# Branch operands, gates and summed weights laid out in DRAM in reading order; branch results added by VectorE; inputs turned beside the first out pair

## The chip, the cores and the metric

One NeuronCore of one Trainium2 chip runs the whole program. It has five engines with queues of their own: TensorE (PE in the profile, its weight loads PEld), VectorE (DVE), ScalarE (ACT), GpSimd (POOL) and SyncE (SP), and 16 DMA engines that they share. SP and POOL issue the transfers. An engine's queue runs in order: an instruction that waits holds up everything behind it. The metric is the device time of one execution in microseconds (us); less is better.

## The reference: what is computed

One layer of a streaming encoder, width 1024, over 1024 prompt frames and 32 sample frames (1056 together), in fp32:

```
z = RMSNorm(x) @ W_in                    # queries, keys, values, gates
y_A = attention(...)                     # windowed, 16 heads
y_B = HGRN2(...)                         # gated linear recurrence, 8 heads
m = sigmoid(gate_A) * (y_A @ W_brA) + sigmoid(gate_B) * (y_B @ W_brB)
x = x + RMSNorm(m @ W_out)
x = x + RMSNorm((gelu(conv3(a)) * u) @ W_down),  [a | u] = RMSNorm(x) @ W_up
x = x + (p @ W_ple) * sigmoid(x @ W_ple_gate)
```

The change touches how `y_A`, `y_B`, the gates and the branch weights get into DRAM and back, the line of `m`, the product with `W_out`, and the transposition of the per-layer input `p`.

## The kernel before

**Numbers.** Activations lie transposed: features on the 128 partitions, frames along the row. Every fp32 product is made of three reduced-precision ones. A value is split into a high part (`hi`, a cast on ScalarE) and what is left (`lo`, a subtraction on VectorE), and PE multiplies hi by hi, hi by lo and lo by hi. `split` and `halves` are these two steps. For the weights of the out projection they make `wh` and `wl` (`load_next`, lines 182 to 189); where ScalarE has time, `lo_by` can be set to "dma" and `lo` is made by ScalarE (minus the weight) and an accumulating transfer on POOL.

**Stages, in order of time.** Attention to about 365 us, the HGRN recurrence to 822, the last gates to 851, branch A (`y_A @ W_brA`) to 938, branch B to 1022.6, the out projection in two pairs to 1076 and 1127.5, the product with `W_ple`, the feed-forward part to 1840, and the end.

**The branches** use a Strassen-like scheme: instead of eight block products seven are made, from sums of blocks. `H` is 264 frames, a quarter of 1056; halves of frames, of features and of columns are named by t, h, a. The sums of activations lie in DRAM (`sa_d`, `sb_d`), the sums of weights too (`wa_d`, `wb_d`). They are made during the HGRN stage by transfers that add on arrival, issued by POOL (`block_sum`, line 1458; `a_sums`, `y_sums`, `b_sums` are 21 of them, and `yb_sum` adds the activations of B by heads). `gate_out` (line 292) writes the gates `ta_d`, `tb_d` as [128, 1056] in frame order, the HGRN output goes to `yb_d` so as well.

`a_unit(br, ph, c)` does one column block of 128: in phase 0 the products i = 0, 1, 2, in phase 1 i = 3 to 6, each with 24 matmuls of 128 x 264 into a PSUM tile `st`. These are 34 steps for A (some are halves) and 28 for B; `beside(n)` runs what `during(step, ...)` has put beside a step: operand loads (`a_load`), splits (`a_split`), weight pieces. `both(...)` puts them behind what ScalarE and VectorE have got already; otherwise a scheduler chooses each engine's order. For i = 2, 4, 5, 6 a result comes out: VectorE subtracts (L1662), and multiplies by the gate (L1664). A's results are written to `mx_d` by POOL (L1669). B's are added to them by an accumulating transfer `ta<-mx_d` (L1671), and three steps later `out_parts` splits the sum into the operands `Ra`, `Rb` of the out projection (L228, L229). Only the last three results have their addend loaded (`ma_load`) and added by VectorE (L1666).

**The out projection.** `W_out` comes in 8 blocks of columns, twice: `p` 0 and 1 are two pairs of frame quarters. `block` makes a bank `mm` with 24 matmuls (L205 to L207), `z_out` scales it and sums its squares (L1796 to L1802). Beside the first pair `early_parts` prepares weights of later stages (`pw`, stored to `pw_d` by POOL). Beside the second pair the first pair's norm and residual are made (L1849 on), and `p_cols` turns `p`: 12 pieces of 88 frames, two PE transposes each into two banks `tr`; after every third piece the two banks are split into `pc` (L228, L229). There are two `tr` banks, so the next group's first transpose waits until these splits have read them. `ple_product` uses the `pc` tiles after the second pair.

## Time and profile before

| | us |
|---|---|
| median of 3 runs | 1959.74 (1958.93 to 1960.01) |
| profiled execution | 1956.43 |
| its span, first to last instruction | 1954.7 |
| mean granted TensorE clock | 0.998 of full |

| stage (us from the span's start) | length | PE busy | DVE busy | ACT busy | POOL busy |
|---|---|---|---|---|---|
| last gates, 822 to 851 | 29.00 | 28.37 | 12.48 | 12.80 | 4.33 |
| second out pair, 1076 to 1127.5 | 51.50 | 48.89 | 40.60 | 33.63 | 6.79 |
| `W_ple` product, 1127.5 to 1160 | 32.50 | 31.86 | 23.59 | 21.11 | 8.61 |

The branches and the first out pair are shown in the prediction. A matmul is named by what it writes and reads (`st<-oa,wt`: into the PSUM tile `st` from the activation `oa` and the weight `wt`); operands of A are `oa`, of B `ob`, a raw weight piece is `wa`, its split `wt`. `DMA_DIRECT2D` on POOL is the issue of a transfer, not the transfer. [...]

### The profile page before, as it was taken

Reading aid. Unit: us, or ns where it says so; the run is one execution under the profiler, and the core shown is the slowest. Engines: PE = TensorE matmul, PEld = TensorE weight load, DVE = VectorE, ACT = ScalarE, POOL = GpSimd, SP = SyncE. Lnnn points to the kernel's source line nnn. Section 1 sums busy time; section 2 is a strip of 40 time slices with the busy share of each in tenths; the row PEclk is TensorE's granted clock in tenths of the full one; section 3 lists DMA queues with packets and bytes.
Section 4 is the critical chain, followed back from the end, with each engine's and each line's share of the span. In section 5 each row is a group of like instructions: output and inputs, shape, how many; then the busy total and the mean of one; then the engine's idle time right before and its main releaser. Section 6 shows DMA issues by size and latency. Waiting matters only on the chain.

```text
span 1954.7 us, 38121 instructions
## 1 busy us (share of the span) xinstructions
PE 1921.2 (98%) x14523; PEld 1901.4 (97%) x14523; DVE 1466.1 (75%) x3189; ACT 1027.3 (53%) x2212; POOL 343.9 (18%) x464
## 2 busy tenths in 40 slices
PE   8999999999999999999999999999999999999998
PEld 8999999999999999999989999999999999999998
DVE  6777777788888888666675878788777786768862
ACT  7667777666666666553435663333333336534432
POOL 2111211010101001101111124354554410000000
PEclk9999999999999999999999999999999999999999
DMA  8544543455547354499988583656988357755442
GB/s 269 149 114 122 132 128 92 143 113 138 146 113 176 111 119 95 126 306 301 279 196 271 175 271 107 184 150 185 178 169 198 107 175 235 220 183 155 117 133 84
DMA packets 332300, 325.62 MB, mean 167 GB/s; under 512 B 17654, under 2 KB 293017, under 8 KB 332118
## 3 DMA queue, kind: packets, MB, share of 16 engines
q1 hardware_dynamic: 290533, 234.61, 39.0%
q0 software_dynamic: 41456, 88.53, 20.6%
q8 instruction: 114, 1.87, 0.4%
q14 instruction: 69, 0.56, 0.1%
q10 hardware_dynamic: 128, 0.06, 0.0%
HBM read 232.58 MB, written 132.20 MB: 187 GB/s over the span
## 4 chain that ended last, share of the span: by engine, by line
PE 39%; issue 5%; DVE 3%; DMA 2%; ACT 1%; POOL 0%; ACTq 0%; POOLq 0%; DVEq 0%; SPq 0%
PE st L2330 7%; PE st L2329 7%; PE st L2328 7%; PE st L2452 4%; PE st L2454 4%; PE st L2453 4%; PE st L205 2%; PE st L206 2%; PE st L207 2%; DMA pw_d<-pw 1%; DMA ta<-mx_d 1%; DVE wt L1996 0%; PE mm L205 0%; PE mm L206 0%; PE mm L207 0%
## 5 line engine op out<-in xcount | busy, mean ns | idle before, releaser
L2328 PE MATMUL st<-op,wt 128*128 128x264 f32 x1232 | 348.8, 283 | 2.8 <-ACT Sp L2339 1.4
L2330 PE MATMUL st<-op,wt 128*128 128x264 f32 x1232 | 349.7, 284 | 0.0
L2329 PE MATMUL st<-op,wt 128*128 128x264 f32 x1232 | 347.7, 282 | 0.0
L2328 PEld LDWEIGHTS st<-op,wt 128*128 128x128 f32 x1232 | 231.2, 188 | 4.6 <-ACT Sp L2339 2.0
L2329 PEld LDWEIGHTS st<-op,wt 128*128 128x128 f32 x1232 | 231.4, 188 | 0.0
L2330 PEld LDWEIGHTS st<-op,wt 128*128 128x128 f32 x1232 | 230.8, 187 | 0.0
L2452 PE MATMUL st<-dop,wt 128*128 128x264 f32 x616 | 174.5, 284 | 1.5 <-ACT S L2467 1.5
L2454 PE MATMUL st<-dop,wt 128*128 128x264 f32 x616 | 174.3, 283 | 0.0
L2453 PE MATMUL st<-dop,wt 128*128 128x264 f32 x616 | 173.9, 282 | 0.0
L1995 ACT CAST wt<-wu 128x512 fp32r<-128x512 f32 x126 | 76.0, 618 | 178.7 <-POOL wu L2004 71.0
L205 PE MATMUL mm<-La,wh 128*128 128x384 f32 (+1 forms) x480 | 158.2, 330 | 0.0
L206 PE MATMUL mm<-Lb,wh 128*128 128x384 f32 (+1 forms) x480 | 155.3, 324 | 0.5 <-DVE Lb L782 0.5
L207 PE MATMUL mm<-La,wl 128*128 128x384 f32 (+1 forms) x480 | 154.9, 323 | 0.1
L1996 DVE TENSOR_TENSOR wt<-wu,wt 128x512 fp32r<-128x512 f32 x126 | 86.4, 694 | 44.9 <-ACT wt L1995 44.9
L2452 PEld LDWEIGHTS st<-dop,wt 128*128 128x128 f32 x616 | 115.6, 188 | 2.2 <-ACT S L2467 1.9
L2453 PEld LDWEIGHTS st<-dop,wt 128*128 128x128 f32 x616 | 115.7, 188 | 0.0
L2454 PEld LDWEIGHTS st<-dop,wt 128*128 128x128 f32 x616 | 115.4, 188 | 0.0
L2101 ACT CAST wt<-wd 128x512 fp32r<-128x512 f32 (+1 forms) x84 | 49.0, 586 | 91.3 <-PE st L2454 69.8
L206 PEld LDWEIGHTS mm<-Lb,wh 128*128 128x128 f32 x480 | 90.4, 189 | 1.6 <-DVE Lb L782 1.4
L207 PEld LDWEIGHTS mm<-La,wl 128*128 128x128 f32 x480 | 90.2, 188 | 0.5 <-DVE wl L757 0.5
L205 PEld LDWEIGHTS mm<-La,wh 128*128 128x128 f32 x480 | 90.2, 188 | 0.2 <-ACT La L779 0.2
L1120 PE MATMUL G<-La,wt 128*128 128x288 f32 x288 | 90.4, 314 | 0.0
(609 smaller groups left out, 6276.7 us busy)
## 6 DMA issues: line engine op xcount, KB each, us to landing
wu<-in_w_up_dram SPq DMA_DIRECT2D x42, 512.0 KB
wu<-in_w_in_dram SPq DMA_DIRECT2D x36, 512.0 KB
w_d<-in_w_down_dram POOLq DMA_DIRECT2D x24, 704.0 KB, 8.5
a_d<-Up SPq DMA_DIRECT2D x22, 528.0 KB
wr<-in_w_in_dram SPq DMA_DIRECT2D x21, 512.0 KB
s_d<-sm SPq DMA_DIRECT2D x40, 264.0 KB
dop<-s_d SPq DMA_DIRECT2D x16, 528.0 KB
wr<-in_w_out_dram SPq DMA_DIRECT2D x16, 512.0 KB
```

The lines of the kernel that those rows point to most:

```text
L205: E.matmul(ps, wh, a, start=first and n == 0, stop=False)
L206: E.matmul(ps, wh, b, start=False, stop=False)
L207: E.matmul(ps, wl, a, start=False, stop=last and n == len(ks) - 1)
L1120: E.matmul(o, wh, x[0][k], start=first and k == 0, stop=False, skip_group_check=True)
L1995: S.copy(t[:, 0], src)
L1996: V.tensor_tensor(t[:, 1], src, t[:, 0].bitcast(F32), op=ALU.subtract)
L2328: E.matmul(o, wh, xh, start=first and k == 0, stop=False, skip_group_check=True)
L2329: E.matmul(o, wh, xl, start=False, stop=False, skip_group_check=True)
L2330: E.matmul(o, wl, xh, start=False, stop=k == 3, skip_group_check=True)
L2452: E.matmul(o, wh, xh_, start=first and k == 0, stop=False, skip_group_check=True)
L2453: E.matmul(o, wh, xl_, start=False, stop=False, skip_group_check=True)
L2454: E.matmul(o, wl, xh_, start=False, stop=k == ng - 1, skip_group_check=True)
```

## The change

Five parts.

1. Layouts. `ya_d`, `yb_d`, `ta_d`, `tb_d`, `sa_d`, `sb_d`, `wa_d`, `wb_d` are indexed in the order in which the branches read them, so that a load takes one run per partition: 4224 B for an operand instead of 4 x 1056, 2112 for a gate instead of 2 x 1056, 2048 for a summed weight piece instead of 4 x 512. Writers pay with more pieces: `gate_out` and the HGRN output write two transfers instead of one, and the weight sums of each branch become 26 transfers instead of 8.
2. Results of B. No accumulating transfer: every result's addend `ma` is loaded by SP about three results ahead, VectorE adds it, and the split stands one step later instead of three.
3. `W_out`. The first two blocks are loaded at steps 55 and 57 and split at 58 and 59 with `lo` by ScalarE and an accumulating transfer; later blocks as before. In the first pair, what `early_parts` makes stands behind what ScalarE and VectorE have by then.
4. The last result. It is made in two halves of frames; the second half now stands behind the first and behind what the queues hold.
5. `p_cols` moves from the second out pair to the first. Groups 2 and 3 come first, go to DRAM (`pc_d`) and are reloaded late in the second pair.

```diff
-    ya_d = dp.tile([P, 8, T], F32, name="ya_d")
-    ta_d = [dp.tile([P, T], F32, name=f"ta_d{i}") for i in range(8)]
+    ya_d, yb_d = (dp.tile([P, 2, 2, 2, 4, H], F32, name=f"y{x}_d") for x in "ab")
+    ta_d, tb_d = ([dp.tile([P, 2, 2, H], F32, name=f"t{x}_d{i}") for i in range(8)] for x in "ab")
...
-    wa_d, wb_d = ({o: dp.tile([P, 4, 512], F32, name=f"w{x}_d{o}") for o in (1, 3, 4, 6)} for x in "ab")
-    sa_d, sb_d = ({o: dp.tile([P, 4, 2, H], F32, name=f"s{x}_d{o}") for o in (1, 3, 4, 5)} for x in "ab")
+    wa_d, wb_d = ({o: dp.tile([P, 4, 4, P], F32, name=f"w{x}_d{o}") for o in (1, 3, 4, 6)} for x in "ab")
+    sa_d, sb_d = ({o: dp.tile([P, 2, 4, H], F32, name=f"s{x}_d{o}") for o in (1, 3, 4, 5)} for x in "ab")
...
-            dma(dst[:, o:o + n], t[:, :n])
+            for a, e in PIECES[g]:
+                q = a // H
+                dma(dst[:, q % 2, q // 2, a % H:a % H + e - a], t[:, a - o:e - o])
...
-        for n, (dst, (o, src, acc)) in enumerate(sums):
-            at(26 + 15 * n // 2, block_sum, dst[o][:], src, acc)
+        def weight_sums(d, v):
+            parts = ((3, 0, 0, 0), (4, 0, 1, 0), (1, 0, 0, 0), (6, 1, 0, 0), (3, 0, 1, 1), (4, 1, 1, 1))
+            r = [(d[o][:, c], v[:, a, h, c], acc) for o, a, h, acc in parts for c in range(4)]
+            return r + [(d[1][:], d[4][:], 1), (d[6][:], d[1][:], 1)]
...
+        for n, a in enumerate(y_sums + weight_sums(wa_d, av) + weight_sums(wb_d, bv)):
+            at(26 + 17 * n // 6, block_sum, *a)
...
-                    for z_ in (slice(0, 1), slice(1, 2)) if last and i == 6 else (sl,):
+                    def result(z_):
...
-                        if last:
-                            V.tensor_tensor(g, g, ma_a[i][:, z_], op=ALU.add)
-                            out_parts(c + 4 * a, h, ta, range(z_.start, z_.stop))
+                        if br:
+                            V.tensor_tensor(g, g, ma[:, z_], op=ALU.add)
+                            if last and i > 4:
+                                out_parts(c + 4 * a, h, ta, range(z_.start, z_.stop))
+                    if last and i == 6:
+                        result(slice(0, 1))
+                        both(result, slice(1, 2))
+                    else:
+                        result(sl)
...
-                    elif not last:
-                        gdma(ta[:], mx_d[:, 2 * a + h, c], accum_op=ALU.add)
-                        during(n_s[0] + 3, both, out_parts, c + 4 * a, h, ta)
+                    else:
+                        if not (last and i > 4):
+                            during(n_s[0] + 1, both, out_parts, c + 4 * a, h, ta)
+                        if mixes:
+                            mix_load()
...
-        during(58, prefetch)
-        during(59, both, load_next)
+        for n in range(2):
+            during(32 + n, mix_load)
+            during(55 + 2 * n, raw_next)
+            during(58 + n, both, load_next)
...
-        g, i = divmod(n, 3)
+        i, g = n % 3, (n // 3 + 2) % 4
...
+            if g > 1:
+                dma(pc_d[g - 2][:], xs[:].bitcast(F32))
...
-                if p and c > 1:
+                if p == 0 and c > 1:
                     with behind(E):
-                        p_cols(2 * c + g - 6)
+                        p_cols(2 * c + g - 4)
```

Where it moves instructions, on the engines that the prediction speaks of:

VectorE at the end of branch B, before the change. `ac` and `e` are results, `st` the PSUM tile of the last product, the numbers behind the names tell tiles apart; L1662 with 128x264 is the subtraction of one half of the last result, L229 makes `Rb`.

```order
L1662 TENSOR_TENSOR ac_13080<-st_12940,Rb__12080 128x264
L1666 TENSOR_TENSOR ta_12901<-ta_12901,ma_12937 128x528
L1664 SCALAR_TENSOR_TENSOR ta_12935<-ta_12935,ac_13080 128x264
L1662 TENSOR_TENSOR ac_13086<-st_12940,Rb__12080 128x264
L229 TENSOR_TENSOR Rb_12148<-ta_12901,Ra_12147 128x264
L229 TENSOR_TENSOR Rb_12150<-ta_12901,Ra_12149 128x264
```

And with the change, the same place (L1667 is the subtraction, L1669 the gate, L1671 the add, L227 `Rb`):

```order
L1671 TENSOR_TENSOR ta_13043<-ta_13043,ma_13077 128x528
L227 TENSOR_TENSOR Rb_12262<-ta_13043,Ra_12261 128x264
L227 TENSOR_TENSOR Rb_12264<-ta_13043,Ra_12263 128x264
L227 TENSOR_TENSOR Rb_12657<-ta_13006,Ra_12656 128x264
L227 TENSOR_TENSOR Rb_12659<-ta_13006,Ra_12658 128x264
L1667 TENSOR_TENSOR e_13218<-st_13088,Rb__12194 128x264
L1669 SCALAR_TENSOR_TENSOR ta_13079<-ta_13079,e_13218 128x264
L1671 TENSOR_TENSOR ta_13079<-ta_13079,ma_13151 128x264
L227 TENSOR_TENSOR Rb_12657<-ta_13079,Ra_12656 128x264
L1667 TENSOR_TENSOR e_13224<-st_13088,Rb__12194 128x264
```

The second read of `st`, which frees the PSUM tile, moved from the second place behind the first read to the fourth, and both moved behind four `Rb` of the two results before.

VectorE in the first out pair with the change, where the second group of `p` pieces is split. `pw` are early weight parts (L2052 their `lo`), `wl` an out weight, `sqz` the sums of squares, `pc` the turned `p` from the banks `tr`.

```order
L2052 TENSOR_TENSOR pw_13307<-rs_13305,pw_13306 128x1024
L184 TENSOR_TENSOR wl_13729<-wr_13726,wh_13728 128x1024
L1809 TENSOR_TENSOR sqz_13243<-sqz_13243,sq_13635 128x264
L2052 TENSOR_TENSOR pw_13306<-rs_13305,pw_13306 128x1024
L227 TENSOR_TENSOR pc_13646<-tr_13559,pc_13646 128x264
L227 TENSOR_TENSOR pc_13646<-tr_13560,pc_13646 128x264
```

The last two rows are new in this place; before, they stood in the second pair, behind the residual steps L1850 and L1913.

## Prediction

> **What bounds the kernel now.** The page comes first. Its first line says that TensorE (PE) works through 98% of the span, so no other engine's total matters; only what makes PE wait can be won.

> ```profile
> PE 1921.2 (98%) x14523; PEld 1901.4 (97%) x14523; DVE 1466.1 (75%) x3189; ACT 1027.3 (53%) x2212; POOL 343.9 (18%) x464
> ```

> Second, the list of who waited for whom, for PE alone and from 840 to 1165 us, where the change works (branch A to about 938, branch B to 1022.6, out projection to 1127.5). The columns are the total wait in us, times, longest.

> ```profile
> PE tr L1952 <- DVE pc L229: 2.5, 1, 2.5
> PE mm L205 <- ACT Ra L228: 2.5, 1, 2.5
> PE st L1640 <- DVE ac L1662: 2.3, 2, 1.5
> PE st L1642 <- DVE ob L1558: 1.5, 1, 1.5
> PE st L1640 <- ACT as L1649: 1.4, 1, 1.4
> ...
> PE st L1640 <- DVE R L1651: 0.9, 1, 0.9
> PE st L1640 <- ACT gt L297: 0.8, 1, 0.8
> PE tr L1822 <- DVE pc L229: 0.6, 1, 0.6
> PE st L1640 <- DVE ac L1654: 0.5, 1, 0.5
> ```

> These rows hold 13.0 us, 0.7% of the span; PE's instructions are the same before and after. So the stake is small, and the question is which rows go and which grow. The windows by stage give the room (columns: PE, PEld, DVE, ACT, POOL busy, granted clock, DMA share, GB/s).

> ```profile
> 851.00:895.00 44.00, 41.50 (x338) 41.09 (x339) 30.79 (x42) 22.46 (x34) 7.09 (x10) 1.00 1.03 305
> 895.00:938.40 43.40, 41.09 (x337) 40.66 (x336) 30.90 (x45) 14.98 (x21) 6.02 (x12) 1.00 0.97 292
> 938.40:1022.60 84.20, 82.18 (x675) 81.58 (x673) 59.29 (x94) 34.03 (x62) 11.98 (x15) 1.00 0.90 233
> 1022.60:1076.00 53.40, 50.88 (x420) 50.91 (x420) 31.77 (x53) 28.85 (x58) 8.21 (x14) 1.00 0.86 272
> 1100.00:1110.00 10.00, 7.47 (x50) 7.26 (x50) 9.40 (x13) 7.97 (x17) 0.75 (x1) 0.83 0.30 92
> ```

> In branch A the transfer engines are full (1.03, 0.97), in the out projection less so.

> **Branch A, weights and operands in reading order.** ScalarE's waits behind the PE rows:

> ```profile
> 882.26 0.62 ACT L228 CAST wt<-wa 128x512 fp32r<-128x512 f32 x1 [6.44 <-DMA wa<-in_w_br_a_dram]
> 909.98 0.62 ACT L228 CAST wt<-wa 128x512 fp32r<-128x512 f32 x1 [5.46 <-DMA wa<-wa_d]
> wa<-wa_d SPq DMA_DIRECT2D x14, 256.0 KB
> ```

> The weight piece comes late because the queue is full; PE waits for what ScalarE then does late (`as` 1.4, `ac` 2.3, together 3.7). How much faster long pieces go is not shown directly. Two microseconds with larger transfers in them are the nearest:

> ```profile
> 1026.00:1028.00 2.00, 2.00 (x19) 2.00 (x18) 2.00 (x5) 0.41 (x1) 0.00 (x0) 1.00 1.08 368
> ```

> 368 against 305 GB/s saves at most 1 - 305/368 = 17%. The summed weights (14 of 0.26 MB) and as many operand loads of 0.54 MB are 11 MB, 37 us at 305 GB/s: at most 6 us of transfer, at least 0. The lateness to be won is 3.7 us, in three places over 30 us. I take all **3.7**, with 0 as the other end, and leave the `R` and `gt` rows (1.7 more at best), since they stand at the start where little has been saved and SP issues the gates in more pieces.

> [...]

> **Branch B, the adds.** Thirteen accumulating transfers `ta<-mx_d` go.

> ```profile
> 980.30 0.73 ACT L228 CAST Ra<-ta 128x264 fp32r<-128x264 f32 x2 [2.66 <-DMA ta<-mx_d]
> 1001.57 0.73 ACT L228 CAST Ra<-ta 128x264 fp32r<-128x264 f32 x2 [3.44 <-DMA ta<-mx_d]
> L1664 DVE SCALAR_TENSOR_TENSOR ta<-ta,ac 128x528 f32<-128x528 f32 x23 | 16.1, 702 | 0.1
> ```

> ScalarE is a queue: while `Ra` waits for the landing, the weight and operand casts behind it wait too, and the PE rows `ob` 1.5 and `ac L1654` 0.5 follow. Now `Ra` waits for a VectorE add of about 0.70 us, and its other operand is loaded three results ahead. VectorE gets 13 x 0.70 = 9.1 us into 24.9 idle (84.2 - 59.3), less two `wl` of 1.2 that leave. Gain **2.0**; 0 if `ob` was late anyway. Those two `wl` of the out weights are now made by ScalarE and an accumulating transfer of the kind that stands in the trace already:

> ```profile
> wl<-wr POOLq DMA_DIRECT2D x11, 512.0 KB, 4.6
> ```

> Issued in the last unit's first step, some 10 us before PE uses them, they land 5 us early: cost 0, and some 5 us if POOL were busy then, which it isn't.

> **The boundary to the out projection.** The first out matmul reuses the last result's PSUM tile, so it waits for the last VectorE read of it (the second half), not for `Ra`, which the view names.

> ```profile
> 1017.58 0.71 DVE L1664 SCALAR_TENSOR_TENSOR ta<-ta,ac 128x528 f32<-128x528 f32 x1
> 1018.32 0.71 DVE L1666 TENSOR_TENSOR ta<-ta,ma 128x528 f32<-128x528 f32 x1
> 1023.26 0.42 DVE L1662 TENSOR_TENSOR ac<-st,Rb__12080 128x264 f32<-128x264 f32 x1
> 1024.56 0.42 DVE L1662 TENSOR_TENSOR ac<-st,Rb__12080 128x264 f32<-128x264 f32 x1
> 1025.12 0.36 PE L205 MATMUL mm<-Ra,wh 128*128 128x264 f32 x1 [2.52 <-ACT Ra L228]
> ```

> PE ended at 1022.60; the read ended at 1024.98. In the changed order that read stands behind four `Rb` subtractions of the previous results and behind the whole first half (subtract, gate, add, split). From PE's end: the previous result's matmuls end 2.9 earlier (24 at 82.18/675 = 0.122); its three dependent 528-wide steps at 0.74 end at -0.6; ScalarE's four casts (0.41, then 0.32 apart) end at 0.8; the last `Rb` at 1.3; the first half's three steps at 0.42 to 0.46 end at 2.4, its cast at 2.9, its `Rb` at 3.4, beside whose end the second half's read runs, to 3.7. So the wait grows from 2.5 to about 3.7 (3.4 if dependent steps overlap more): **+1.2**.

> A long wait also costs clock. After the 2.53 us wait at 1103.97 TensorE runs below full clock for a while (the window 1100 to 1110 above, granted clock 0.83):

> ```profile
> 1103.97 0.37 PE L1952 MATMUL tr<-ident,pr 88*128 88x88 f32 x2 [2.53 <-DVE pc L229]
> ```

> By the clock 0.17 of 10 us, 1.7, are lost; by the matmuls, 50 in 7.47 us where 0.122 each would give 61, 1.3. I use 1.5. The 2.52 us wait at 1025 drew none, so about 2.5 us is where it turns on how the wait falls; 3.7 is well past that, and I add **+1.5** (0 at the other end).

> [...]

> **Second out pair.** The transposes of `p` leave it.

> ```profile
> 1101.15 1.26 DVE L1850 TENSOR_TENSOR x<-x,z 128x1056 f32<-128x1056 f32 x1 [0.60 <-DMA x<-xt_d]
> 1102.32 1.25 DVE L1913 TENSOR_TENSOR z<-z,z 128x1056 f32<-128x1056 f32 x1
> 1103.49 0.77 DVE L229 TENSOR_TENSOR pc<-tr,pc 128x264 fp32r<-128x264 f32 x2
> ```

> The next transposes wait until these `pc` steps have read the bank, and they stand behind 2.5 us of normalisation that a transfer made late. Without them 2.5 + 1.5 go, and some 0.4 of the 0.6 at `tr L1822`, whose sums stood behind a `pc` step: **-4.4**. The banks of this pair (six) are read by ScalarE, so nothing else is next; the two reloads of `pc` are needed only at 1127.

> **First out pair.** The 24 transposes, 8 casts and 8 subtractions arrive here; VectorE and ScalarE have over 20 us idle each, but order matters. At the second change of group the two `pc` subtractions stand behind the 1.2 us `pw` step, which waits for a store of `pw` that ScalarE released about 1 us before.

> ```profile
> L2040 DVE TENSOR_TENSOR pw<-rs,pw 128x1024 fp32r<-128x1024 f32 x2 | 2.4, 1220 | 3.8 <-ACT pw L2038 3.8
> DMA to landing us min/median/max: 2.9/5.2/9.0
> ```

> PE reaches the next transposes 34 matmuls later, 4.2 us. Issue 1.2 us early, landing 2.9 to 5.2, then 1.2 + 0.8 of VectorE: ready after 3.7 to 6.0. I take a wait of **+0.8**; with the longest landing it is 5.6, and never below nothing.

> **HGRN stage.** The weight sums become 52 small transfers on POOL instead of 16 (57 against 21 with those of `y`). They hide: state loads are issued early.

> ```profile
> 777.49 0.59 POOL L1326 DMA_DIRECT2D S<-in_state_hgrn_dram  x1 [19.03 <-PE so L1371]
> 784.20 0.39 PE L1371 MATMUL so<-S,tq 128*128 128x128 f32 x2
> DMA to landing us min/median/max: 2.1/2.1/2.3
> L1458 POOL DMA_DIRECT2D wa_d<-wa_d x2 | 1.9, 932 | 7.7 <-DMA wa_d<-wa_d 7.7
> ```

> A load is in use 6.7 us after its issue and lands in 2.1: 4.6 of slack. Cost 0, as long as no sum that waits for another sum stands directly ahead.

> **Sum.** -3.7 - 2.0 + 1.2 + 1.5 - 4.4 + 0.8 = -6.6 us. The profiled execution took 1956.4 (span 1954.7, 1.7 around it), 3.3 below the median of the runs, 1959.7. From 1956.4 it gives 1949.8; set against the median, **1953.1**.

> **Rivals.** (1) Long pieces win nothing: branch A's row stays, 1956.8. [...] (2) The first pair only inherits the second's trouble: a landing of 7.5 us makes its wait 4 and draws half clock: 3.2 + 1.5 more, 1957.8. For it: landings up to 9.0 in just this stage; against it: they shorten to about 3 late in the pair. (3) Slower: POOL's sums in series. One that waits 7.7 for its forerunner directly ahead of a state load makes PE 7.7 - 4.6 = 3.1 late; it decides from four of the eight heads on: 12.4 us, 1965.5. Against it: the order puts these chains some 20 us ahead of the loads. (4) The first rows don't go because the accumulates were not what held ScalarE: 2.0 less, 1955.1, inside the forecast.

> **Chances.** Forecast 0.56, (1) 0.18, (2) 0.14, (3) 0.08, others slower 0.04. About 0.2%, 3.9 us, is what a measurement tells from no change, so "faster" ends at 1955.8: the forecast and little of the rivals, 0.58; the rest of (1) and (2), 0.30; slower 0.12. The range: without the clock loss, the least first-pair wait and the `R` row, 6.6 + 1.5 + 0.8 + 0.9 = 9.8 less than the median gives 1949.9, and 1 us below for what isn't named; above, (1) and (2) together would be 1961.5, so I stop at 1960.5.

> **What would show it.** Right: no PE wait over 0.3 us for `as` or `ac` in branch A; ScalarE never waits for `ta<-mx_d`; the wait at the first out matmul is 3.4 to 4 with a clock below 1 behind it; none for `pc` after 1076, one of about 1 before it. Wrong: a boundary wait at 2.5 or less, waits in branch A as before, or POOL waiting ahead of a state load.

## The result, and the profile after

The changed kernel is slower. Its median is 1969.77 us (lowest 1967.12, five runs) against 1958.93 us of the kernel before on the same chip (1955.05 to 1960.01, five runs). The ratio is 1.0059, with a 95% interval of 1.0042 to 1.0075; one disturbed run of 2675.38 us is left out of it. The profiled execution took 1967.12 us, its span 1965.4, against 1956.4 and 1954.7 before: 10.7 us more, where the prediction had 6.6 less.

The page's first line still says that TensorE does the same work (1924.7 us against 1921.2, 14523 matmuls both times):

```profile
PE 1924.7 (98%) x14523; PEld 1903.0 (97%) x14523; DVE 1474.1 (75%) x3200; ACT 1029.7 (52%) x2214; POOL 364.3 (19%) x489
```

So the time lies in waits again. The list of who waited for whom, for PE over the whole span (total, times, longest):

```profile
PE mm L203 <- DVE e L1667: 4.0, 1, 4.0
PE st L1643 <- DVE ac L1667: 2.8, 1, 2.8
...
PE st L1643 <- DVE ac L1657: 2.1, 1, 2.1
PE st L1643 <- ACT as L1652: 2.0, 3, 1.1
PE Y L1122 <- DVE vt L1143: 2.0, 1, 2.0
PE tr L1959 <- DVE pc L227: 1.9, 2, 1.5
PE st L1643 <- ACT wt L226: 1.8, 1, 1.8
...
PE tr L1959 <- DMA pr<-in_p_sample_dram: 1.1, 1, 1.1
```

The reader is to see three things: the rows of branch A (`st` from `ac`, `as`, `wt`) did not go but grew, there is a new row in the HGRN stage (`Y`, 0.6 before), and the transposes of `p` (`tr L1959`) wait in their new place too. The windows by stage (PE, PEld, DVE, ACT, POOL busy, clock, DMA share, GB/s) add the clock, below 1 in branch A and in the first out pair:

```profile
357.00:854.00 497.00, 492.95 (x3278) 489.54 (x3277) 402.67 (x1111) 309.28 (x789) 77.89 (x118) 1.00 0.55 130
854.00:948.00 94.00, 84.69 (x672) 83.31 (x672) 62.23 (x87) 38.24 (x56) 12.47 (x20) 0.98 0.93 291
948.00:1034.00 86.00, 82.03 (x675) 81.64 (x674) 70.96 (x117) 37.59 (x68) 3.63 (x5) 0.99 0.78 236
1034.00:1096.00 62.00, 58.47 (x458) 57.50 (x459) 30.66 (x49) 30.55 (x63) 7.44 (x13) 0.95 0.79 262
```

Measured from the first matmul of each stage to that of the next, in us:

| stage | before | after | difference | predicted |
|---|---|---|---|---|
| HGRN | 493.5 | 496.9 | +3.4 | 0 |
| branch A | 87.3 | 94.3 | +6.9 | -3.7 |
| branch B, with the wait at the first out matmul | 86.6 | 85.9 | -0.7 | -0.8 |
| first out pair | 52.5 | 61.9 | +9.4 | transposes, +0.8, clock +1.5 |
| second out pair | 51.7 | 43.5 | -8.2 | transposes, -4.4 |
| out projection to up projection, pairs included | 132.0 | 134.1 | +2.1 | -2.1 |

The transposes that change sides are 24 matmuls, some 2.7 us. The stages around these make the rest, about 1 us less in sum. Each length is that of one profiled execution: in two kernels that differ only behind branch B (before, and the run with the move of `p` alone below) branch A was 87.3 and 88.8 us, so a stage difference of 1.5 us or less is not told by one profile.

### The profile page after: what moved, and what is told of

Its sections match the earlier page's. It is cut to its first block, busy times and chain, and to the rows that moved or that the text cites. A ratio compares the mean times of both kernels' runs of the same rounds, so it can differ in the third digit from the quotient of the medians.

```text
span 1965.4 us, 38289 instructions
## 1 busy us (share of the span) xinstructions
PE 1924.7 (98%) x14523; PEld 1903.0 (97%) x14523; DVE 1474.1 (75%) x3200; ACT 1029.7 (52%) x2214; POOL 364.3 (19%) x489
## 5 line engine op out<-in xcount | busy, mean ns | idle before, releaser
L2007 ACT CAST wt<-wu 128x512 fp32r<-128x512 f32 x126 | 75.9, 618 | 179.4 <-POOL wu L2016 72.0
L205 PE MATMUL mm<-La,wl 128*128 128x384 f32 (+1 forms) x480 | 155.0, 323 | 0.1
L2008 DVE TENSOR_TENSOR wt<-wu,wt 128x512 fp32r<-128x512 f32 x126 | 86.4, 694 | 46.7 <-ACT wt L2007 46.7
L205 PEld LDWEIGHTS mm<-La,wl 128*128 128x128 f32 x480 | 90.3, 188 | 0.5 <-DVE wl L759 0.5
L1043 ACT CAST wt<-wu 128x512 fp32r<-128x512 f32 x108 | 65.2, 617 | 48.6 <-DVE wu L1051 24.2
## 6 DMA issues: line engine op xcount, KB each, us to landing
wu<-in_w_up_dram SPq DMA_DIRECT2D x42, 512.0 KB
wu<-in_w_in_dram SPq DMA_DIRECT2D x36, 512.0 KB
wr<-in_w_in_dram SPq DMA_DIRECT2D x21, 512.0 KB
wr<-in_w_out_dram SPq DMA_DIRECT2D x16, 512.0 KB
```

What stands on the lines that cost most here:

```text
L205: E.matmul(ps, wl, a, start=False, stop=last and n == len(ks) - 1)
L2007: S.copy(t[:, 0], src)
L2008: V.tensor_tensor(t[:, 1], src, t[:, 0].bitcast(F32), op=ALU.subtract)
```

## The experiments

"Before" is the kernel before, "changed" the changed one; each edit is to the one that is named. All times are ratios to the kernel before on the same chip, with 95% intervals. Stages are measured as in the table.

**First: which parts cost.** The gate tiles `ta` share memory with the new tiles `ma`, so their ring went from 8 to 6 tiles. A gate load has to wait until the mixed gate that lay in its tile has been written to `mx_d`. SP issues these loads between the weight pieces, and its waits in branch A (850 to 946 us) nearly doubled, before and after:

```profile
SPq L1609 <- DMA mx_d<-ta: 17.5, 5, 5.8
```

```profile
SPq L1605 <- DMA mx_d<-ta: 32.2, 9, 7.7
```

*The short ring on the kernel before.*

```diff
-                t = mp.tile([P, 2, H], F32, tag="ta", name=nm("ta"), bufs=8)
+                t = mp.tile([P, 2, H], F32, tag="ta", name=nm("ta"), bufs=6)
```

> The kernel before, with nothing changed but the ring of gate tiles (ta) cut from 8 to 6, as in the change. Theory R (ring): a gate load on SP must wait until the result that used its tile six loads earlier has landed in DRAM; with 6 tiles it comes to that wait two results earlier, and the weight pieces queue behind it on SP. It expects branch A to grow from 87.4 us to 92 or more, of the 94.3 that the change shows, and the kernel to be 4 to 7 us slower than before (1.002 to 1.0036). Rival L (layout): the long pieces fill the transfer queues and delay the weight pieces whatever the ring; it expects branch A within 1 us of 87.4 and no change of the time.

Measured: 1.0027 (1.0013 to 1.0041), branch A 96.1 us, as theory R has it. Two tiles less are enough to make branch A of the kernel before 8.8 us longer.

*A longer ring on the changed kernel:* `ta` and `ma` in one ring.

```diff
-                t = mp.tile([P, 2, H], F32, tag="ta", name=nm("ta"), bufs=6)
+                t = mp.tile([P, 2, H], F32, tag="ta", name=nm("ta"), bufs=9)
...
-            ma_a.append(mp.tile([P, 2, H], F32, tag="ma", name=nm("ma"), bufs=3))
+            ma_a.append(mp.tile([P, 2, H], F32, tag="ta", name=nm("ma"), bufs=9))
```

> The changed kernel with the gate tiles and the addends (ma) sharing one ring of 9 tiles, which is the same memory as 6 and 3. In branch A no addends are used, so the gates have 9. Theory R expects branch A at 88 us or less instead of 94.3 and the kernel about 6 us faster than the change, 1.0027 to 1.004 against before. Rival L expects branch A at 94 as before this edit and no gain.

Measured: 1.0042 (1.0029 to 1.0055), branch A 89.8 us, SP's waits for mixed-gate writes 18.0. So the ring holds some 4.5 of branch A's 6.9 us, but not all of them: PE's waits in the branch fell from 9.3 to 6.5 us, and one stretch at half rate (last section), worth 1.5 us, is gone (granted clock 1.00 from 928 to 936 us, 0.79 in the changed kernel).

*The last result of branch B in its own place.* The changed kernel issues the second half of the last result behind everything that ScalarE and VectorE have been given so far.

```diff
-                        both(result, slice(1, 2))
+                        result(slice(1, 2))
```

> The changed kernel with the second half of the last result written directly behind the first, not held behind what the queues have. Its read of the PSUM tile then stands next to the first half's. Theory C (order and clock): the wait at the first out matmul falls from 3.95 to about 2.1 us and the half clock behind it (24 matmuls, 2.4 us) is gone or down to half of that; 3 to 4.5 us faster than the change. Rival: the wait goes, but the clock is lost anyway because of the other waits in this stage; 1.9 faster at most.

Measured: 1.0050 (1.0037 to 1.0064). The wait at the first out matmul fell from 3.95 to 2.11 us as expected, and branch B with it by 1.9; yet 15 matmuls at half rate still followed, and the first pair stayed at 61.5 us. The place of the last result is the wait's cause; the half rate shrank with it from 25 matmuls to 15 and did not go, and longer waits for `p` took that back. The time is 1.8 us below the changed kernel's, as the rival has it.

*The sums put back.* The change runs the first five sums (of `y`) closer together.

```diff
-        for n, a in enumerate(y_sums + weight_sums(wa_d, av) + weight_sums(wb_d, bv)):
-            at(26 + 17 * n // 6, block_sum, *a)
+        for n, a in enumerate(y_sums):
+            at(26 + 15 * n // 2, block_sum, *a)
+        for n, a in enumerate(weight_sums(wa_d, av) + weight_sums(wb_d, bv)):
+            at(63 + 9 * n // 4, block_sum, *a)
```

> The changed kernel with the sums spread as before: the five sums of y at the spacing they had, the 52 weight sums behind them. Theory S: in the change the second sum of y (0.5 MB, accumulating) was issued at 351 us, where it delays the first loads of HGRN, and the last weight sums at 788 and 799 delay the loads of La; it expects the waits at 365, 388 and 800 us (3.4 together) to fall to about 0.6 as before, 2.5 us faster than the change. Rival: these waits come from the gates' and outputs' extra pieces; no gain.

Measured: 1.0035 (1.0023 to 1.0047), HGRN 495.2 us. In the changed kernel the second sum goes out at 351 us, lands after 14.2 us and holds up SP's weight pieces, which PE then waits for. In its timeline (start, duration, line, transfer) and the list of its issues:

```profile
351.18 0.90 POOL L1452 DMA_DIRECT2D sa_d<-ya_d  x1 [17.31 <-issue]
356.82 14.65 SPq L1031 DMA_DIRECT2D wu<-in_w_in_dram  x4
sa_d<-ya_d POOLq DMA_DIRECT2D x1, 1056.0 KB, 14.2
```

Before, and in this run, no sum starts between 340 and 395 us, the four issues take 11.2 and 11.4 us, and PE's wait at `Y` is 0.6 us. What remained was a wait of 1.2 us at 800 us; the last weight sum goes out at 775 us in this run, so the wait's cause is not shown.

**Second: parts alone.** *Gate loads by POOL instead of SP* (changed kernel, ring of 6).

```diff
-                dma(t[:, z_], src[c_][:, h_, z_])
+                gdma(t[:, z_], src[c_][:, h_, z_])
```

> The changed kernel with the gate loads issued by POOL's queue, behind the mixed-gate writes, and no longer by SP between the weight pieces; the ring stays at 6. If the short ring costs its time by holding SP's queue (SP waited 32.2 us in branch A for landings of mixed-gate writes, before 17.5), the weight pieces go out on time: the stretch of branch A falls from 94.3 to 87-90 us, ACT waits for weight pieces at most 25 us in all there (34.8 in the changed kernel, 35.3 before with waits that PE did not feel), and the time falls by 4 to 7 us, a ratio of 1.0025 to 1.004. If the gates themselves come too late from a ring of 6, whoever issues them, branch A stays at 93 us or more and the waits of PE for the gated product stay.

Measured: 1.0075 (1.0063 to 1.0087), branch A 91.1 us, between the two expectations, but the HGRN stage 501.2. ScalarE's waits for weight pieces fell to 22.1 us, but PE waited 3.2 us at the branch's first matmul (counted in the HGRN stage) and 5.1 us at 894. The run tells nothing apart: it freed SP and put new waits on POOL.

*Part 1 alone on the kernel before:* the layout and its sums, with the ring of 8, the accumulating writes and the old place of `p`. The diff is the one in the section on the change, without parts 2 to 5.

> The kernel before with part 1 alone: operands, gates and summed weights kept in reading order, with the sums cut and placed as in the change; the ring of 8, the accumulating writes and the place of the p columns are those of before. If long pieces win nothing in branch A and the sums cost where they now run (transfers of 512 bytes took 29.2 ns, of 2048 bytes 113.7): the HGRN stretch grows by 2.5 to 4 us (493.5 to 496-497.5), branch A stays within 1.5 us of 87.4, and the ratio is 1.001 to 1.002. If the prediction's first term was right and only the ring hid it: branch A 84.5 us or less, and the ratio 0.999 or less unless the HGRN stretch takes it back.

Measured: **1.0079** (1.0066 to 1.0092), HGRN 498.9 us, branch A 93.4. The layout alone, with a ring of 8, costs at least about as much as the whole change (1.0059); the two intervals overlap, so that the other parts give some of it back is not shown. Neither expectation had branch A at 93. Its timeline shows how, POOL first:

```profile
890.93 0.59 POOL L1663 DMA_DIRECT2D mx_d<-ta  x1 [10.71 <-DVE ta L1658]
891.51 0.93 POOL L1451 DMA_DIRECT2D sb_d<-sb_d  x1
901.61 0.87 POOL L1451 DMA_DIRECT2D sb_d<-sb_d  x1 [9.17 <-DMA sb_d<-sb_d]
902.17 0.90 POOL L1663 DMA_DIRECT2D mx_d<-ta  x1
```

The last sum of branch B's operands (`sb_d`, at 901.61) adds to what the sum before it wrote, so POOL waits 9.2 us for that landing, and the mixed gate behind it is written only at 902.17. SP's issues:

```profile
901.79 0.39 SPq L1524 DMA_DIRECT2D wa<-in_w_br_a_dram  x1
902.22 0.50 SPq L1524 DMA_DIRECT2D wa<-wa_d  x1
902.82 8.60 SPq L1603 DMA_DIRECT2D ta<-ta_d  x2
911.51 0.38 SPq L1548 DMA_DIRECT2D ob<-sb_d  x1
911.99 0.86 SPq L1524 DMA_DIRECT2D wa<-wa_d  x2
```

The second gate load of the row at 902.82 needs that write's landing and holds SP until 911.1; the weight pieces behind it leave at 911.99. ScalarE waits for them, and PE for ScalarE, at half rate afterwards (0.22 us from one matmul to the next, not 0.12):

```profile
917.57 0.62 ACT L225 CAST wt<-wa 128x512 fp32r<-128x512 f32 x1 [7.77 <-DMA wa<-wa_d]
919.68 0.56 PE L1634 MATMUL st<-oa,wt 128*128 128x264 f32 x1 [3.28 <-ACT wt L225]
920.03 0.42 PE L1636 MATMUL st<-oa,wt 128*128 128x264 f32 x1
920.25 0.42 PE L1638 MATMUL st<-oa,wt 128*128 128x264 f32 x1
```

*The columns of `p` back beside the second pair* (changed kernel; its hunks on `p_load`, `p_cols` and `pc_load` undone).

> The changed kernel with the input's columns turned beside the second out pair again, as before, without the round through DRAM. If the move gains what its two stretches show apart from the half clock at the boundary (the second pair lost 8.2 us, of which 2.7 are the transposes; the first gained 9.4, of which 2.7 are the transposes and 2.4 the half clock): first pair 54 to 56.5 us, second pair 51 to 52.5, and the time 1 to 3 us above the changed kernel's, a ratio of 1.0065 to 1.0075. If the first pair took the trouble along (waits of 3.5 us for columns and input pieces that were 2.5 in the second pair): the two pairs together are within 1 us of the changed kernel's 105.5 and the ratio stays at 1.0055 to 1.0063.

Measured: 1.0062 (1.0049 to 1.0075), first pair 55.1 us, second 53.2, together 108.3 against 105.5, while the ratio does not differ from that of the changed kernel. In the trace the move wins what was said (2.8 us); in the time it can't be seen.

**Third: the chain, and the move alone.** *The loads of part 1 cut into the old pieces* (`max_dma_last_dim` bounds one piece, in bytes: between 851 and 940 us SP's queue moved 29796 packets with it, 15085 without).

```diff
-            dma(t[:, 4 * a:4 * a + 4], src[:, c])
+            dma(t[:, 4 * a:4 * a + 4], src[:, c], max_dma_last_dim=512)
...
-        queue(opa[b, i, p][:, 1].bitcast(F32), src[:, p])
+        queue(opa[b, i, p][:, 1].bitcast(F32), src[:, p], max_dma_last_dim=1056)
...
-                dma(t[:, z_], src[c_][:, h_, z_])
+                dma(t[:, z_], src[c_][:, h_, z_], max_dma_last_dim=1056)
```

> The kernel with part 1 alone, but with the loads of weights, operands and gates in the branches cut into the pieces of before again (512 and 1056 bytes instead of 2048, 4224 and 2112); what lies in DRAM, the sums and their order stay. If the long pieces are what holds POOL's transfers back (its summing transfers took 7.2 and 7.7 us to land before, 8.8 and 9.5 in long pieces; the writes of mixed gates 5.7 and 6.3), these medians come back to within 0.5 us of before and branch A falls from 93.4 to 87-89.5 us. If it is the order and number of the transfers around them, the medians stay above 8.3 and 9 us and branch A at 92 us or more.

Measured: 1.0060 (1.0047 to 1.0072), branch A 92.0 us. The issue list gives the median time to landing of POOL's sums (last number) before, with part 1 alone, and with the old pieces:

```profile
sb_d<-yb_d POOLq DMA_DIRECT2D x2, 264.0 KB, 7.7
sb_d<-sb_d POOLq DMA_DIRECT2D x2, 264.0 KB, 7.2
```

```profile
sb_d<-yb_d POOLq DMA_DIRECT2D x2, 264.0 KB, 9.5
sb_d<-sb_d POOLq DMA_DIRECT2D x2, 264.0 KB, 8.8
```

```profile
sb_d<-yb_d POOLq DMA_DIRECT2D x2, 264.0 KB, 7.8
sb_d<-sb_d POOLq DMA_DIRECT2D x2, 264.0 KB, 7.8
```

With long pieces on SP's queue these transfers of POOL's queue take longer to land, 9.5 and 8.8 us against 7.8 and 7.8, as expected; why is not shown. The first of the two was 8.5 to 9.6 us in five profiles with long pieces (changed kernel, four places undone, part 1 alone, with the last sum later, with the gates kept as before) and 7.7 to 7.8 in three with short ones (kernel before, with the last sum later, cut pieces). But the landings are not what made branch A long, which is where the second expectation has it: it got only 1.4 us shorter, the writes of mixed gates did not get faster (5.8 us), and PE's waits in the branch grew from 7.6 to 8.7 us. What went are the two windows at half rate (granted clock of the execution 0.997, with part 1 alone 0.995).

*The last sum later.* The same kernel (part 1 alone) with one number changed.

```diff
-            during(12 + n, yb_sum, n, 3)
+            during((12, 13, 14, 22)[n], yb_sum, n, 3)
```

> The kernel with part 1 alone, but the last of POOL's four sums of branch B's operands in branch A is issued at step 22 instead of 15, behind the writes of mixed gates that it stood ahead of. If the chain is: the sum waits on POOL for the landing of the sum before it, the write of the mixed gate waits behind it, SP waits for that write's landing (7.8 us the longest) and holds the weight pieces: SP's waits for mixed-gate writes fall from 19.8 us in all to 12 or less, branch A from 93.4 to 89-91.5 us and the ratio by 0.001 to 0.002. If SP is held as long by its load of the third sum (5.5 us), which stands ahead of these gates: branch A falls by less than 1 us.

Measured: 1.0030 (1.0018 to 1.0042), branch A **88.2** us. POOL's timeline at the same place:

```profile
890.02 0.94 POOL L1451 DMA_DIRECT2D sb_d<-sb_d  x1
895.96 0.58 POOL L1663 DMA_DIRECT2D mx_d<-ta  x1 [5.00 <-DVE ta L1658]
```

The mixed gate is written 6 us earlier and waits for VectorE alone. In this run one step of order on POOL takes back 5.2 of the 6 us that part 1 cost in branch A; 2.1 came back in branch B (a wait of 2.3 us for an operand's split, half rate behind it). Not as expected: SP's waits for these writes fell by only 0.7 us in all (to 19.1), but the longest from 7.8 to 6.0. The ratio fell by 0.0049, more than was expected and far more than the 1.9 us between the two profiled executions; what the step is worth in the whole time stays open between these.

*The move of `p` alone on the kernel before.* The diff is that of the change on `p_load`, `p_cols` and `pc_load`.

> The kernel before with part 4 alone: the input's columns turned beside the first out pair, two of the four groups through DRAM. If the prediction's two terms for it hold (second pair 4.4 us less, first pair 0.8 more, and 2.7 us of transposes that change sides): second pair 43.5-45 us, the stretch from the first out pair to the up stage 128 to 130 us (132.0 before), ratio 0.998 to 0.9992. If the first pair takes the trouble along: that stretch at 131 us or more, ratio within 0.0008 of 1.

Measured: 1.0001 (0.9990 to 1.0012), second pair 43.5 us, first 61.6, the stretch to the up stage 133.7 us, of which some 1.5 us are half rate after a boundary wait of the same 2.5 us. The first pair took the trouble along, as rival (2) says:

```profile
PE tr L1953 <- DMA pr<-in_p_prompt_dram: 4.7, 3, 2.5
```

Two tiles for the pieces, a piece used every 3.1 us, and 5.6 to 7.3 us from issue to landing for the three that PE waited for (the first left SP at 1045.78 and landed at 1053.11): the load cannot keep ahead.

*Four places undone in the changed kernel:* ring of 9, last result in place, sums of `y` back and weight sums at `63 + 41 * n // 20`, last sum at step 22.

> The changed kernel with the four places undone that the traces point to: gate and mixed-gate tiles share a ring of 9, the sums of y stand where they stood and the weight sums end at piece 167 instead of 184, the last of POOL's four sums of branch B's operands comes at step 22, and the last out part is issued in its place. If their costs add (each measured or read alone: the ring 4.5 us of branch A, the sums about 3, the last out part 1.8, the last sum 2): 8 to 11 us below the changed kernel, a ratio of 1.0005 to 1.002. If they are one queue of DMA work that only moves, less than 6 us below, a ratio of 1.003 or more.

Measured: 1.0035 (1.0022 to 1.0048), about 4.7 us below the changed kernel: the gains don't add. That is the second expectation. Branch A stayed at 91.7 us, HGRN got a wait of 2.3 us at 747, and the first pair grew to 67.0 with this row, where the casts of `p` stood on ScalarE behind an out weight that had come late:

```profile
PE tr L1961 <- DVE pc L227: 5.4, 1, 5.4
```

**Fourth: what is left, and a version that beats both.** *The last sum later on the kernel before.* The diff is the one above.

> The kernel before with one edit: the last of POOL's four sums of branch B's operands in branch A at step 22 instead of 15. If the chain over POOL's queue costs the short-piece kernel too (there the write of a mixed gate went out at 894.51 us behind a sum that waited for 893.70, SP waited 3.97 us for its landing, and PE 0.84 and 1.47 us soon after): branch A falls from 87.4 to 84.5-86.5 us and the ratio is 0.998 to 0.9995. If only long pieces make the sums late enough: branch A within 0.7 us of 87.4, ratio within 0.0008 of 1.

Measured: 0.9994 (0.9985 to 1.0003), branch A 86.8 us, inside the second expectation. In short pieces the chain cost 0.5 us of branch A in these two profiles, too little for the time or one profile to show.

*Part 1 alone with the last sum later and the sums put back.*

> Part 1 alone, with the last sum at step 22, the sums of y at their old places and the weight sums 2.25 pieces apart. If the layout's costs are these two (branch A 5.2 us with the one, HGRN 1.7 to 3 with the other): HGRN 495-496.5 us, branch A 87.5-89, ratio 0.9995 to 1.0015, no better than before though its transfers in branch A take 8 us less of each DMA engine. If the layout costs something of its own in the HGRN stretch: ratio 1.002 or more with HGRN at 497 us or more.

Measured: 1.0026 (1.0016 to 1.0035). HGRN is as short as before, 494.1 us. Branch A is not, 92.4: a wait of 2.9 us at its second bank, 2.6 at 904, each with half rate behind it. SP's issues ahead of the first of these:

```profile
850.21 0.90 SPq L299 DMA_DIRECT2D tb_d<-gt  x2
851.28 0.42 SPq L1550 DMA_DIRECT2D oa<-sa_d  x1
851.80 1.19 SPq L299 DMA_DIRECT2D tb_d<-gt  x2
853.10 0.52 SPq L1605 DMA_DIRECT2D ta<-ta_d  x1
853.99 0.38 SPq L1526 DMA_DIRECT2D wa<-in_w_br_a_dram  x1
```

Each gate output leaves in two transfers, because the reading order cuts it; ScalarE had the weight piece of 853.99 only at 860.05, 6.1 us later, where it was 3.8 in the kernel before.

*The same with the gates kept as before.*

```diff
-            for a, e in PIECES[g]:
-                q = a // H
-                dma(dst[:, q % 2, q // 2, a % H:a % H + e - a], t[:, a - o:e - o])
+            dma(dst[:, o:o + n], t[:, :n])
```

> The kernel of the run sum_late_spread (part 1 with the last sum at step 22 and the sums at their old places), but the gates are written and kept as before: one transfer for each output, and loads in pieces of 1056 bytes. If the gates' split writes at the start of branch A are the rest of the layout's cost: PE's wait for the copy of branch A's second bank (2.87 us at 862) falls to 1.2 us or less, its half clock goes, branch A falls from 92.4 to 87.5-89.5 us and the ratio from 1.0026 to 1.0015 or less. If the long operand and weight pieces themselves cost the rest: branch A stays at 91 us or more, the ratio at 1.002 or more.

Measured: 1.0011 (1.0001 to 1.0021), branch A **86.5** us. Its waits there:

```profile
PE st L1634 <- DVE ac L1656: 2.6, 1, 2.6
PE st L1634 <- ACT gt L296: 0.8, 1, 0.8
```

The wait at the second bank is gone, as the first expectation has it. With all three costs of the layout out of the way, branch A is as long as with short pieces and the late sum (86.8). What the long pieces save is in the DMA queues of the two, as a share of 16 engines, short pieces over 86 us first:

```profile
q1 hardware_dynamic: 29466, 21.49, 82.5%
q0 software_dynamic: 1904, 4.60, 18.6%
```

```profile
q1 hardware_dynamic: 17245, 21.46, 74.8%
q0 software_dynamic: 2160, 4.60, 19.6%
```

That is 101.1% against 94.4% of 86 us: 5.8 us of transfer saved, 0.3 us of time won. PE's waits in the branch are 1.4 us less (2.6 against 4.0), but the wait of 2.6 us drew a window at half rate, 1.5 us, where the other run has none (granted clock 0.998 and 0.999). In the five profiles with the kernel before's layout and ring these waits lie between 3.1 and 4.6 us, so long pieces win 0.5 to 2 us of waiting by this, and one such window takes it back. Still longer than before are the HGRN stage (495.9 us, 2.4 more, with a wait of 1.2 us at 801) and branch B (1.5 more).

*Half of `p` in each pair* (kernel before with the move, one piece beside each row block instead of two, in both pairs; the edit is to the run with the move alone).

```diff
-                if p == 0 and c > 1:
+                if c > 1 and g % 2:
                     with behind(E):
-                        p_cols(2 * c + g - 4)
+                        p_cols(6 * p + c - 2)
```

> The kernel before with half of the input's columns turned in each out pair, one piece beside every output row block (some 7 us apart) instead of two. If the first pair lost because two input tiles cannot be loaded in 3.3 us each (PE waited 2.47, 0.67 and 1.54 us for them): no wait over 0.6 us for input pieces in the first pair, the second pair's wait of 2.53 us gone, the stretch from the first out pair to the up stage 127.5 to 130 us (132.0 before), ratio 0.998 to 0.9995. If the pairs lose for another reason (DVE or the clock): 131 us or more, ratio within 0.0008 of 1.

Measured: 0.9997 (0.9989 to 1.0006). The waits for input pieces are gone and the second pair keeps 0.7 us of its wait, but the first has one of 2.9 us for the columns' split, with 15 matmuls at half rate, and the stretch to the up stage is 135.3 us, as the second expectation has it. The reason was the load in the run with the move alone, and VectorE's order in this one (the casts of `pc` ended at 1059.5 us, its subtractions began at 1060.54, behind an out weight's `wl`).

*Both edits on the kernel before.*

> Both edits on the kernel before: half of the columns in each pair, and the last sum at step 22. If they add: 3 to 7 us below before, a ratio of 0.9965 to 0.9985. If, as in the run with four places undone, what is won at one place is waited for at the next: ratio 0.9993 or more.

Measured: **0.9984** (0.9975 to 0.9993), median 1955.20 against 1957.52 us: the one version whose interval lies below 1. This is in the range expected if the edits add; the two single runs make 0.9991 together, inside the interval. Branch A 86.4 us, and a wait of 1.8 us instead of 2.9 in the first pair. There is one window at half rate between 850 and 1135 us, at 1126.8, as there is one in the kernel before, at 1105.6 (granted clock of both executions 0.998).

## Why the prediction was wrong

**"Branch A ... I take all 3.7, with 0 as the other end"**: this step failed. The other end was no bound: the change could make branch A longer, and it did by 6.9 us. The estimate of the transfers held: "at most 6 us of transfer", 5.8 measured in the last run of part 1. What failed is the step from transfers to PE's wait. The weight piece was late not only because the engines were full, but because SP issued it behind a gate load that waited for a mixed-gate write, which on POOL waited behind a sum. The changed kernel's own trace has the whole of it once: the last sum, waiting for the one before it, held POOL to 898.42 us, the mixed gate behind it landed at 908.03, the gate load that needed this held SP until then, the weight piece behind that left at 909.40, ScalarE cast it at 915.77, and PE's wait of 1.8 us ended at 917.87. The change lengthened that chain at three places that the prediction took no price for: the ring of 6 (4.5 us by the run with 9), the last sum in front of the write (5.2 us with the layout alone, removed by one step of order; the slower landing by itself did not do it, as the cut pieces show), and the split gate writes ahead of the first weight piece (5.9 us in the run that undid them). These overlap: they add to far more than 6.9, and the step of order alone, without the gates' part, left branch A at 88.2 us in one run and 92.4 in another. How much each has of the 6.9 us is not shown: no run undoes the gates' part on the changed kernel itself, and windows at half rate, 1.5 us each, come and go with how a wait falls. The prediction counted VectorE's and SP's instructions, yet not what the smaller ring makes SP wait for.

**"HGRN stage ... Cost 0"**: failed. It looked at state loads and their slack of 4.6 us, which held: no wait at them. The sums collided with weight pieces instead: of the 3.4 us, 2.2 are the waits at 365 and 388 us that went with the sums at their old places. The stage was then still 0.6 to 2.4 us longer than before (494.1 to 495.9 in four runs), which waits of 1.2 us at 800 or 2.3 at 747 explain in part. The condition that was named ("no sum that waits for another sum stands directly ahead") was looked for in the wrong stage: it decided in branch A.

**"Branch B, the adds ... Gain 2.0"**: right. The rows `ob` and `ac` of 1.5 and 0.5 are gone, and none took their place; with part 1 alone, which keeps the accumulating transfers, they stood at 1.7 and 1.5. The size is luck in part: in the run with the move of `p` alone, whose branch B is that of the kernel before, they held 0.3 us.

**"The boundary ... +1.2" and the clock "+1.5"**: the wait was right, 2.5 to 3.95 (+1.4). The half rate was larger, 25 matmuls at 0.22 us, some 2.5 us.

**"Second out pair -4.4"** was right, and **"first out pair +0.8"** was mis-sized: 3.5 us of waits, 1.9 for `pc`, where 0.8 was foreseen, and 1.6 for input pieces that came late, which no term held. The move alone measured 1.0001, so rival (2) describes it: the pair inherits the trouble.

**The rivals.** (1), long pieces win nothing, came close (1.4 us less waiting, 0.3 us of time) and was too kind, since it had nothing to lose by them. For the weights the pieces nearly bear it out: in branch A of the changed kernel a piece of 512 bytes took 29.2 ns on average, one of 2048 bytes 113.7, so four short ones 3% more. (3) named POOL's sums in series as the way to be slower, at the wrong place and with the wrong one waiting.

Of the signs that were to show it, "ScalarE never waits" and the boundary's 3.4 to 4 us came as said; "waits in branch A as before", named as the sign of being wrong, came too, and longer.

Still open: why the wait at branch A's second bank was 1.3 us in one run with split gate writes and 2.9 in another; and a wait for `ac` at 901 to 908 us, 1.3 to 3.1 us long, that stayed in all runs with the layout but the one with gate loads on POOL. Behind it ScalarE waited for a weight piece: in the last run of part 1 it left at 890.02 us and landed 9.4 us later, where the one of the kernel before took 7.7, so there it was the transfers that were slow and not the issue; why is not shown.

## What to carry to other kernels

Where one queue issues loads for several consumers, the time of a load is set by the longest wait ahead of it in that queue (with part 1 alone SP held at a gate load from 902.82 to 911.1 us, and the weight pieces behind it left at 911.99); before a change to sizes or rings, follow that chain to its first wait, and ask of every ring that shrinks whose queue will wait for its release. Less transfer time need not be worth anything by itself, even with the engines at 100%: here 5.8 us of it were 0.3 us of time. Waits undone one by one need not add: in the run with four places undone, what was won at one place was waited for at the next, so a sum of terms needs a run with all of them.

## What the runs showed of the hardware

```profile
927.00:930.41 3.41, 1.43 (x11) 1.46 (x12) 3.41 (x6) 1.22 (x2) 0.54 (x1) 1.00 0.86 277
930.41:933.82 3.41, 3.41 (x18) 3.41 (x17) 2.35 (x4) 0.33 (x1) 0.54 (x1) 0.50 0.92 223
933.82:937.23 3.41, 3.41 (x30) 3.41 (x29) 2.24 (x4) 1.86 (x3) 0.54 (x1) 1.00 0.79 277
```

Here is the start, not at the end of a wait (928.98) but 1.4 us later:

```profile
930.17 0.28 PE L1643 MATMUL st<-oa,wt 128*128 128x264 f32 x1
930.29 0.31 PE L1645 MATMUL st<-oa,wt 128*128 128x264 f32 x1
930.41 0.41 PE L1647 MATMUL st<-oa,wt 128*128 128x264 f32 x1
930.62 0.42 PE L1643 MATMUL st<-oa,wt 128*128 128x264 f32 x1
```

The window at half rate holds 18 matmuls where the next has 30; 12 at 0.12 us are the 1.5 us by which one such window is counted above.

Cutting these two traces between 850 and 1125 us along the steps and adding PE's waits in each window: none of the 156 windows at full rate with up to 1.64 us of waiting was followed by half rate; the three with more, 1.75 us (kernel before), 1.98 and 2.81 us (changed kernel), were. Of the four windows at half rate, the one with 1.15 us of waiting was followed by another, the three with none by full rate. In the kernel before, the boundary's wait of 2.52 us lay across two windows, 1.11 us in the one and 1.41 in the next, and both were followed by full rate; the wait of 2.53 us that ended at 1103.97 had 1.75 us in one window, and half rate followed. So waits of nearly the same length cost some 1.5 us more in one place and nothing in the other.

**Pieces.** In branch A, on SP's queue, pieces of 512 bytes took 29.2 ns and of 2048 bytes 113.7 (changed kernel), next to nothing saved; of 1056 bytes 53.4 (kernel before) and of 4224 bytes 186.8 (changed kernel), an eighth saved. They shorten the engines' work, and the landings of POOL's sums went from 7.7 and 7.2 us (kernel before) to 9.5 and 8.8 (part 1 alone).
